# First projections of a decoder-layer kernel: three units side by side, loads in small pieces, and the norm's factor used later

## The chip, the core and the metric

The kernel runs on one core of a Trainium2 chip. The metric is the device time of one execution in microseconds (us). The profile names the engines of a core PE (TensorE, matrix products; PEld are its weight loads), DVE (VectorE), ACT (ScalarE), POOL (GpSimd) and SP (SyncE, which issues the DMA transfers here). Each engine works through its own queue of instructions in a fixed order, and waits where an instruction needs something that another engine or a transfer has not finished.

## What is computed

One inference step of a decoder layer over 336 tokens (16 meta tokens, a prompt of 256, and 8 sequences of 8 tokens), in float32, with a model width of 2048. Cut to what the change touches:

```python
h = rms_norm(x, norm_w)                  # x * rsqrt(mean(x * x) + eps) * norm_w
proj = h @ w_in
z, xbc, dt_raw, sc_b, sc_c, sc_h, sc_z, g_a, g_b = split_proj(proj)
# branch A: causal conv on xbc, chunked state-space scan, gated norm, projection
...
# branch B: short gated convolution
u = sc_c * sc_h
u_c, sconv_new = causal_dwconv(u, sconv_prev, sconv_w)
y_b = (sc_b * u_c * jax.nn.silu(sc_z)) @ w_sconv_out
merged = jax.nn.sigmoid(g_a) * y_a + jax.nn.sigmoid(g_b) * y_b
return x + merged @ w_o, conv_new, state, sconv_new      # then a final rms_norm
```

The change lies in the norm and in the first projections of branch B: sc_b, sc_c, sc_h and sc_z.

## The kernel before

Tokens lie along the columns, features along the 128 partitions. `ya` holds x as 16 tiles (index k) of 128 features by 336 tokens. A *unit* is a projection onto 128 output features: 16 tiles of k, and for each k three products of 128 by 128 weights with up to 336 columns, since float32 factors are split into a high part that PE multiplies in one pass (fp32r) and the low rest: high times high, high times low, low times high. The weights of a unit are two blocks of 128 by 1024; `wblk` loads a block (SP, `wraw`), makes its high part (ACT, `whi`, L83) and its low part (DVE, `wlo`, L85), with three buffers for each. `unit` and `mm` (L88 to L102) issue for each block eight pairs of products with `whi` (L91, L92), and behind them the eight with `wlo` (L95). `w2[j]`, `w2[16+j]`, `w2[32+j]` and `w2[48+j]` are the weights of the units of sc_b, sc_c, sc_h and sc_z.

Of PSUM there are two buffers named `pj`, for units, and two named `ms`, for small sums. The instructions' order on each engine is set by a scheduler when the program is built, from the order in which the code is written and from its own estimates; buffers of pools are reused in turn, and a tile waits until its buffer is free.

The stage that the change touches, in the order of the code (L147 to L258):

- The vectors `V` (192 KB: conv weights, biases, norm weights) are loaded, the pieces of x, and the blocks of the units w2[16] and w2[32]. POOL halves two parts of `V` (L158, L159).
- x times the norm weight, without the norm's factor, is split into `uhi` (ACT, L163) and `ulo` (DVE, L164). Units on `uhi` and `ulo` need no norm factor ahead of them; their results are multiplied by it afterwards.
- Units w2[16] and w2[32] run side by side over k (L166 to L174). `conv_in` copies the first (`c_s`) and multiplies it with the second into `up`.
- The squares of `ya` (ACT, L214) are summed in `sacc` over k by DVE (L216). `rstd` (L107 to L126) adds up over the partitions with three products on `sacc` (L113); DVE and POOL form the inverse root; DVE lays it on diagonals `rs_d` (L123) and three products (L124) spread it to all partitions. From this come `rsb` (ACT, L226) and its square `rs2` (L228).
- Six more units follow on `uhi` and `ulo`, in this order: w2[48], w2[0], w2[17], w2[33], w2[49], w2[1]. `scaled` multiplies the results of w2[48] and w2[49] (`zf`) and of w2[0] and w2[1] (`bf`) by `rsb` (L231); w2[17] is multiplied by `rs2` where it is copied (L184).
- `ya` becomes h itself (L242) and is split into `hhi` (ACT, L243) and `hlo` (DVE, L244). Everything behind works on these.
- The loop over j (L250 to L258) runs the convolution of branch B (`conv_out`) and splits its result. For j = 0 and 1 the units are done already; from j = 2 on they are computed on `hhi` and `hlo`, the first being w2[18].

## Time and profile before

| | |
|---|---|
| median of 3 runs | 1886.39 us (1881.93 to 1890.16) |
| profiled execution | 1888.47 us, span on the core 1886.5 us |
| mean granted clock of PE | 0.994 of full speed |
| busy share of the span | PE 98%, PEld 96%, DVE 61%, ACT 40%, POOL 17% |
| first 9.2 us of the span | PE busy 0.06 us, DMA share 0.77, 255 GB/s |
| 9.2 to 15.4 us | PE busy 5.85 of 6.20 us, DMA share 1.00, 413 GB/s |

Busy time counts instructions at work; an engine that waits for another is idle. In the lists that follow a row has its start in us, its length, the engine, the line, the operation, the tile written and the tiles read, and in brackets how long the engine had been idle and who ended that. "x8" is a run of eight instructions that follow each other.

### The profile page before, as it was taken

How to read it: one execution, taken by the hardware profiler on the slowest of the kernel's cores; microseconds unless marked ns; L12 is line 12 of the kernel's file. 1: busy time of each engine (PE TensorE's matmuls, PEld its weight loads, DVE VectorE, ACT ScalarE, POOL GpSimd, SP SyncE). 2: the span in 40 equal slices, each digit the busy share in tenths (PEclk: the TensorE clock that was granted, in tenths of full speed). 3: DMA queues.
4: the chain of work that ended last, by engine and by line, in shares of the span. 5: the costliest groups of instructions: out<-in, count | busy, mean ns of one | idle time of the engine just before them, and what ended most of it. 6: DMA issues, size and time to landing. Idle time of an engine off the chain costs nothing.

```text
span 1886.5 us, 31941 instructions
## 1 busy us (share of the span) xinstructions
PE 1848.2 (98%) x12830; PEld 1808.8 (96%) x12830; DVE 1150.8 (61%) x1798; ACT 749.9 (40%) x1050; POOL 313.8 (17%) x397
## 2 busy tenths in 40 slices
PE   7999999999999999999999999999999999999996
PEld 7999999999999999999999999999999999999996
DVE  6844444444534336568586876868778687674543
ACT  5433333333333335444453443534435344233432
POOL 0100000000000002131332323222133221300011
PEclk9999999999999999999999999999999999999998
DMA  6444444444444446456464665646656466575553
GB/s 218 139 155 146 148 153 146 147 156 149 145 158 155 157 163 223 155 174 238 151 236 164 204 207 161 234 152 214 205 169 227 138 212 203 169 258 164 176 170 108
DMA packets 108948, 332.26 MB, mean 176 GB/s; under 512 B 12288, under 2 KB 30336, under 8 KB 108800
## 3 DMA queue, kind: packets, MB, share of 16 engines
q1 hardware_dynamic: 108800, 330.22, 53.5%
q8 instruction: 101, 1.65, 0.4%
q14 instruction: 47, 0.39, 0.1%
HBM read 297.29 MB, written 32.88 MB: 175 GB/s over the span
## 4 chain that ended last, share of the span: by engine, by line
PE 62%; DVE 2%; issue 1%; DMA 1%; ACT 0%; POOL 0%; DVEq 0%; ACTq 0%; SPq 0%
PE pj L91 19%; PE pj L92 19%; PE pj L95 19%; PE yb L541 1%; DMA W<-ac_d 1%; PE ms L520 1%; PE sg L482 1%; DVE wlo L85 1%; DVE W L457 1%; PE ms L439 1%; PE sg L545 0%; PE sg L541 0%; PE ms L124 0%; PE ms L594 0%; DVE cacc L378 0%
## 5 line engine op out<-in xcount | busy, mean ns | idle before, releaser
L91 PE MATMUL pj<-hhi,whi 128*128 128x320 f32 (+3 forms) x2960 | 892.8, 313 | 0.3 <-DVE ya L626 0.3
L92 PE MATMUL pj<-hlo,whi 128*128 128x320 f32 (+3 forms) x2960 | 888.3, 312 | 0.0
L85 DVE TENSOR_TENSOR wlo<-wraw,whi 128x1024 fp32r<-128x1024 f32 x481 | 598.6, 1245 | 458.9 <-PE pj L95 263.2
L83 ACT ACTIVATE whi<-wraw 128x1024 fp32r<-128x1024 f32 x481 | 508.9, 1058 | 846.1 <-PE pj L92 764.9
L91 PEld LDWEIGHTS pj<-hhi,whi 128*128 128x128 f32 x2960 | 557.6, 188 | 5.7 <-issue 3.3
L92 PEld LDWEIGHTS pj<-hlo,whi 128*128 128x128 f32 x2960 | 556.9, 188 | 0.3
L95 PE MATMUL pj<-hhi,wlo 128*128 128x320 f32 (+3 forms) x2960 | 501.4, 312 | 0.0
L95 PEld LDWEIGHTS pj<-hhi,wlo 128*128 128x128 f32 x2960 | 455.8, 188 | 0.3
L91 PE MATMUL pj<-yh,whi 128*128 128x320 f32 x512 | 156.9, 319 | 0.0
L92 PE MATMUL pj<-yl,whi 128*128 128x320 f32 x512 | 152.2, 309 | 0.0
L91 PEld LDWEIGHTS pj<-yh,whi 128*128 128x128 f32 x512 | 96.5, 188 | 7.8 <-issue 5.9
L92 PEld LDWEIGHTS pj<-yl,whi 128*128 128x128 f32 x512 | 96.4, 188 | 1.4 <-issue 1.4
L95 PE MATMUL pj<-yh,wlo 128*128 128x320 f32 x512 | 95.9, 310 | 0.0
L378 DVE SCALAR_TENSOR_TENSOR cacc<-pad,V,cacc 128x360 f32<-128x360 f32 (+1 forms) x144 | 85.0, 590 | 7.4 <-ACT cacc L376 5.6
L626 DVE TENSOR_TENSOR ya<-ya,pj 128x320 f32<-128x320 f32 x112 | 54.2, 484 | 52.7 <-PE pj L95 51.6
L490 POOL TENSOR_TENSOR h<-h,decS 128x512 f32<-128x512 f32 x64 | 72.3, 1166 | 57.3 <-PE ms L520 57.3
L194 POOL COPY SCS<-up 128x2 f32<-128x2 f32 x16 | 19.4, 1215 | 370.9 <-DVE up L188 367.9
L95 PEld LDWEIGHTS pj<-yh,wlo 128*128 128x128 f32 x512 | 80.4, 188 | 0.0
L92 PE MATMUL pj<-vlo,whi 128*128 128x320 f32 x256 | 75.5, 309 | 0.0
L91 PE MATMUL pj<-vhi,whi 128*128 128x320 f32 x256 | 75.5, 309 | 0.0
L371 POOL COPY pad<-cs 128x24 f32<-128x24 f32 x48 | 40.5, 844 | 132.6 <-DVE cacc L378 104.9
L457 DVE TENSOR_SCALAR W<-W,act 128x128 f32<-128x128 f32 (+1 forms) x192 | 54.2, 336 | 6.8 <-DMA W<-ac_d 6.7
(206 smaller groups left out, 1517.9 us busy)
## 6 DMA issues: line engine op xcount, KB each, us to landing
wraw<-w SPq DMA_DIRECT2D x352, 512.0 KB, 3.9
wraw<-wso SPq DMA_DIRECT2D x64, 512.0 KB, 3.5
wraw<-wsc SPq DMA_DIRECT2D x32, 512.0 KB, 3.7
h<-h0T SPq DMA_DIRECT2D x32, 512.0 KB, 5.0
ssms<-h SPq DMA_DIRECT2D x32, 512.0 KB, 4.8
wraw<-wo SPq DMA_DIRECT2D x32, 512.0 KB, 3.8
W<-ac_d SPq DMA_DIRECT2D x16, 512.0 KB, 5.4
xq_d<-xe SPq DMA_DIRECT2D x16, 320.0 KB, 3.5
```

The lines of the kernel that those rows point to most:

```text
L83: nc.scalar.activation(hi[:, :n], raw[:, :n], AF.Copy)
L85: nc.vector.tensor_tensor(lo[:, :n], raw[:, :n], fb(hi[:, :n]), sub)
L91: nc.tensor.matmul(out, w, xh(k0 + k), start=first and k == 0, stop=False)
L92: nc.tensor.matmul(out, w, xl(k0 + k), start=False, stop=False)
L95: nc.tensor.matmul(out, w, xh(k0 + k), start=False, stop=last and k == nk - 1)
L194: nc.gpsimd.tensor_copy(SCS[:, j, 0, :], up[:, 256:258])
L371: nc.gpsimd.tensor_copy(smp[:, :, 0:3], cs[:, 1:9, :])
L378: nc.vector.scalar_tensor_tensor(acc[:, i0:], pad[:, i0 + k:360 + k], col(V_CW, 4 * j + k), acc[:, i0:], mult, add)
L439: nc.tensor.transpose(pp[:n, t * P:t * P + P], xs[:, t, t0:t0 + n], ident)
L457: nc.vector.tensor_scalar(w[:n, h, :n], w[:n, h, :n], act[:n, c, 8 * g + h:8 * g + h + 1], 0.0, sub, ALU.min)
L490: nc.gpsimd.tensor_tensor(split(h0[b]), split(h0[b]), bc(hv(decS[:, b, :], g), [P, 8, HP]), mult)
L626: nc.vector.tensor_tensor(ya[:, m, :TV], ya[:, m, :TV], pp[:, :TV], add)
```

## The change

- *Dummy products.* A tile `warm` is cleared by DVE; ACT reads it once, which loads ACT's function table; PE runs eight products of 128 columns on it into a bank of `ms`.
- *Loads.* Of `V` only the 16 columns of the norm weights come first (8 KB); then a tile of x (168 KB) and 256 columns (128 KB) of each of three blocks, and so on in pieces that grow to two tiles of x and 512 columns. The other parts of `V` come behind all of these. The blocks are split in the same pieces (`wsplit`).
- *Three units side by side.* w2[16], w2[32] and w2[48] run side by side over k; for each k stand the three products of each unit. The third unit's sum lies in a bank of `ms`.
- *Squares.* POOL instead of DVE adds the squares into `sacc`.
- *The factor later.* `rstd` is stopped behind its column sums and the inverse root, the units w2[17] and w2[33] are written ahead of its second half, and w2[0] ahead of its first. w2[48] and w2[0] are copied from PSUM without the factor (ACT) and multiplied in place afterwards (DVE). `up` of the second pair is formed without the factor and multiplied by `rs2` afterwards, as that of the first was.
- *`hlo`.* Every third one is made by POOL instead of DVE (five of 16).

```diff
@@ -22,6 +22,7 @@
 NH = 64
 HP = 64
 EPS = 1e-6
+WARM = 8
 NSTEP = 22
 
 C_ID, C_U, C_M1, C_UQ, C_M1Q, C_ONE = 0, 128, 256, 384, 464, 544
@@ -145,43 +146,68 @@
     CH = ((0, P), (P, P), (2 * P, 80))
 
     with tc.tile_pool(name="pa", bufs=2) as pa:
-        nc.sync.dma_start(V, vec)
-        nc.sync.dma_start(ya[:, 0:2, :], xT[:, 0:2, :])
-        wb = [[wblk(w2[16][:, 0:1024])], []]
-        nc.sync.dma_start(ya[:, 2:4, :], xT[:, 2:4, :])
-        nc.sync.dma_start(ya[:, 4:8, :], xT[:, 4:8, :])
-        wb[1].append(wblk(w2[32][:, 0:1024]))
-        nc.sync.dma_start(ya[:, 8:12, :], xT[:, 8:12, :])
-        wb[0].append(wblk(w2[16][:, 1024:2048]))
-        nc.sync.dma_start(ya[:, 12:16, :], xT[:, 12:16, :])
-        wb[1].append(wblk(w2[32][:, 1024:2048]))
-        nc.gpsimd.tensor_scalar(V[:, V_CW:V_CW + 240], V[:, V_CW:V_CW + 240], 0.5, None, mult)
-        nc.gpsimd.tensor_scalar(V[:, V_SCW:V_SCW + 48], V[:, V_SCW:V_SCW + 48], 0.5, None, mult)
+        warm = pa.tile([P, 256], F32, name="warm", bufs=1)
+        nc.vector.memset(warm, 0.0)
+        nc.scalar.activation(warm[:, 0:1], warm[:, 1:2], AF.Copy)
+        pw = ps.tile([P, 512], F32, name="ms")
+        for _ in range(WARM):
+            nc.tensor.matmul(pw[:, :P], warm[:, P:], warm[:, :P], start=True, stop=True)
         uhi = pa.tile([P, KT, T], F32R, name="uhi", tag="vhi", bufs=1)
         ulo = pa.tile([P, KT, T], F32R, name="ulo", tag="vlo", bufs=1)
+        first = [(w2[16], 14), (w2[32], 14), (w2[48], META)]
+        wb = [tuple(wp.tile([P, 1024], d, name=n) for n, d in (("wraw", F32), ("whi", F32R), ("wlo", F32R)))
+              for _ in first]
+        pu = [ps.tile([P, 512], F32, name=n) for n in ("pj", "pj", "ms")]
+
+        def lw(a, b):
+            for (src, _), (raw, hi, lo) in zip(first, wb):
+                o = slice(a % 1024, a % 1024 + b - a)
+                nc.sync.dma_start(raw[:, o], src[:, a:b])
+
+        def lx(a, b):
+            nc.sync.dma_start(ya[:, a:b, :], xT[:, a:b, :])
+
+        def wsplit(a, b):
+            for raw, hi, lo in wb:
+                o = slice(a % 1024, a % 1024 + b - a)
+                nc.scalar.activation(hi[:, o], raw[:, o], AF.Copy)
+                nc.vector.tensor_tensor(lo[:, o], raw[:, o], fb(hi[:, o]), sub)
+
+        nc.sync.dma_start(V[:, V_NW:V_NW + KT], vec[:, V_NW:V_NW + KT])
+        lx(0, 1)
+        lw(0, 256)
+        lx(1, 2)
+        lw(256, 512)
+        lx(2, 4)
+        lw(512, 1024)
+        lx(4, 6)
+        lx(6, 8)
+        edge = {0: (0, 256), 2: (256, 512), 4: (512, 1024), 8: (1024, 1536), 12: (1536, 2048)}
         for k in range(KT):
             nc.scalar.activation(uhi[:, k, :], ya[:, k, :], AF.Copy, scale=col(V_NW, k))
             nc.vector.scalar_tensor_tensor(ulo[:, k, :], ya[:, k, :], col(V_NW, k), fb(uhi[:, k, :]), mult, sub)
-
-        pu = [ps.tile([P, 512], F32, name="pj") for _ in range(2)]
-        for half in range(2):
-            for k in range(8):
-                for i in range(2):
-                    hi, lo = wb[i][half]
-                    kk = 8 * half + k
-                    for j, (w, x) in enumerate(((hi, uhi), (hi, ulo), (lo, uhi))):
-                        nc.tensor.matmul(pu[i][:, :T - 14], w[:, k * P:k * P + P], x[:, kk, 14:],
-                                         start=kk == 0 and j == 0, stop=kk == 15 and j == 2)
+            if k in edge:
+                wsplit(*edge[k])
+            if k in (4, 8):
+                lx(k + 4, k + 6)
+                lw(*edge[k + 4])
+                lx(k + 6, k + 8)
+            for (_, t0), p, (raw, hi, lo) in zip(first, pu, wb):
+                for j, (w, x) in enumerate(((hi, uhi), (hi, ulo), (lo, uhi))):
+                    o = k % 8 * P
+                    nc.tensor.matmul(p[:, :T - t0], w[:, o:o + P], x[:, k, t0:],
+                                     start=k == 0 and j == 0, stop=k == 15 and j == 2)
+        nc.sync.dma_start(V[:, 0:V_NW], vec[:, 0:V_NW])
+        nc.sync.dma_start(V[:, V_NW + KT:], vec[:, V_NW + KT:])
+        nc.gpsimd.tensor_scalar(V[:, V_CW:V_NW], V[:, V_CW:V_NW], 0.5, None, mult)
+        nc.gpsimd.tensor_scalar(V[:, V_SCW:V_SCW + 48], V[:, V_SCW:V_SCW + 48], 0.5, None, mult)
 
         def uproj(src, t0):
             return unit(src, lambda k: uhi[:, k, t0:T], lambda k: ulo[:, k, t0:T], T - t0)
 
-        def conv_in(j, pr, pre=None, fac=None):
+        def conv_in(j, pr, pre=None):
             c_s = pa.tile([P, T - 14], F32, name="c_s")
-            if fac is None:
-                nc.scalar.activation(c_s, pre[0] if pre else pr(w2[16 + j], 14), AF.Copy)
-            else:
-                nc.vector.tensor_tensor(c_s, pr(w2[16 + j], 14), fac, mult)
+            nc.scalar.activation(c_s, pre[0] if pre else pr(w2[16 + j], 14), AF.Copy)
             ph = pre[1] if pre else pr(w2[32 + j], 14)
             up = pa.tile([P, 338], F32, name="up")
             ups = eights(up[:, 258:338], 10)
@@ -207,13 +233,13 @@
                                     mult)
             return th
 
-        up0, ups0 = conv_in(0, None, [p[:, :T - 14] for p in pu])
+        up0, ups0 = conv_in(0, None, [p[:, :T - 14] for p in pu[:2]])
         sacc = pa.tile([P, T], F32, name="sacc", bufs=1)
         for k in range(KT):
             sq = pa.tile([P, T], F32, name="sq") if k else sacc
             nc.scalar.activation(sq, ya[:, k, :], AF.Square)
             if k:
-                nc.vector.tensor_tensor(sacc, sacc, sq, add)
+                nc.gpsimd.tensor_tensor(sacc, sacc, sq, add)
 
         def consts(a, b):
             craw = wp.tile([P, 1024], F32, name="craw", tag="wraw")
@@ -221,19 +247,26 @@
             nc.vector.tensor_copy(CR[:, a:b], craw[:, :b - a])
 
         consts(0, C_SE)
-        rs = run(rstd(pa, [sacc], 0, 1.0 / DM, EPS))
+        zf = [pa.tile([P, TV], F32, name="zf", bufs=1)]
+        nc.scalar.activation(zf[0], pu[2][:, :TV], AF.Copy)
+        bf = [pa.tile([P, TV], F32, name="bf", bufs=1)]
+        nc.scalar.activation(bf[0], uproj(w2[0], META), AF.Copy)
+        norm = rstd(pa, [sacc], 0, 1.0 / DM, EPS)
+        next(norm)
+        up1, ups1 = conv_in(1, uproj)
+        rs = run(norm)
         rsb = pa.tile([P, T], F32, name="rsb", bufs=1)
         nc.scalar.activation(rsb, rs, AF.Copy)
         rs2 = pa.tile([P, T], F32, name="rs2", bufs=1)
         nc.vector.tensor_tensor(rs2, rsb, rs, mult)
+        for f in (zf[0], bf[0]):
+            nc.vector.tensor_tensor(f, f, rsb[:, META:], mult)
+
         def scaled(w, name, **kw):
             f = pa.tile([P, TV], F32, name=name, **kw)
             nc.vector.tensor_tensor(f, uproj(w, META), rsb[:, META:], mult)
             return f
 
-        zf = [scaled(w2[48], "zf", bufs=1)]
-        bf = [scaled(w2[0], "bf", bufs=1)]
-        u1 = conv_in(1, uproj, fac=rs2[:, 14:])
         zf.append(scaled(w2[49], "zf1", tag="sq"))
         bf.append(scaled(w2[1], "bf1", tag="sq"))
         nc.sync.dma_start(SCS, sconvst)
@@ -241,14 +274,15 @@
             hf = ya[:, k, :]
             nc.vector.scalar_tensor_tensor(hf, hf, col(V_NW, k), rsb, mult, mult)
             nc.scalar.activation(hhi[:, k, :], hf, AF.Copy)
-            nc.vector.tensor_tensor(hlo[:, k, :], hf, fb(hhi[:, k, :]), sub)
-        nc.vector.tensor_tensor(up0[:, :258], up0[:, :258], rs2[:, 14:272], mult)
-        nc.vector.tensor_tensor(ups0[:, :, 2:10], ups0[:, :, 2:10], eights(rs2[:, 272:]), mult)
+            (nc.gpsimd if k % 3 == 2 else nc.vector).tensor_tensor(hlo[:, k, :], hf, fb(hhi[:, k, :]), sub)
+        for u_, us in ((up0, ups0), (up1, ups1)):
+            nc.vector.tensor_tensor(u_[:, :258], u_[:, :258], rs2[:, 14:272], mult)
+            nc.vector.tensor_tensor(us[:, :, 2:10], us[:, :, 2:10], eights(rs2[:, 272:]), mult)
 
         vhi = pa.tile([P, KT, TV], F32R, name="vhi", bufs=1)
         vlo = pa.tile([P, KT, TV], F32R, name="vlo", bufs=1)
         for j in range(KT):
-            u = (up0, ups0) if j == 0 else u1 if j == 1 else conv_in(j, proj)
+            u = (up0, ups0) if j == 0 else (up1, ups1) if j == 1 else conv_in(j, proj)
             if j == 3:
                 nc.sync.dma_start(HV, hvec)
                 consts(C_SE, C_ALL)
```

How the order on the engines changes. PE before, from the end of the first pairs of products of w2[0] on (`sacc` holds the summed squares, `rs_d` the factor's diagonals):

```order
L91 MATMUL pj<-uhi,whi 128x320
L92 MATMUL pj<-ulo,whi 128x320
L113 MATMUL ms<-CR,sacc 112x1 x3
L95 MATMUL pj<-uhi,wlo 128x320 x5
L124 MATMUL ms<-rs_d,CR 128x112 x2
L95 MATMUL pj<-uhi,wlo 128x320 x2
L124 MATMUL ms<-rs_d,CR 128x112
L95 MATMUL pj<-uhi,wlo 128x320
L91 MATMUL pj<-uhi,whi 128x320
```

PE now, from the end of the three units on, and, in the second list, around the use of the factor:

```order
L198 MATMUL pj<-uhi,wlo 128x322
L198 MATMUL ms<-uhi,whi 128x320
L198 MATMUL ms<-ulo,whi 128x320
L198 MATMUL ms<-uhi,wlo 128x320
L114 MATMUL ms<-CR,sacc 112x1 x3
L92 MATMUL pj<-uhi,whi 128x320
L93 MATMUL pj<-ulo,whi 128x320
```

```order
L92 MATMUL pj<-uhi,whi 128x322
L93 MATMUL pj<-ulo,whi 128x322
L96 MATMUL pj<-uhi,wlo 128x322 x8
L125 MATMUL ms<-rs_d,CR 128x112 x2
L92 MATMUL pj<-uhi,whi 128x320
L93 MATMUL pj<-ulo,whi 128x320
```

The column sums stand right behind the three units now, ahead of all of w2[0]; before they stood behind its first 16 products. Between them and the first use of `rs_d` lie now the units w2[0], w2[17] and w2[33] instead of five products. The third product on `rs_d` stands two pairs further on.

POOL before, behind its start, and now:

```order
L158 ISA
L158 TENSOR_SCALAR V<-V 128x240
L159 TENSOR_SCALAR V<-V 128x48
L193 COPY up<-SCS 128x8x2 x2
L118 TENSOR_TENSOR rs_r<-rs_m,mhalf 112x3
```

```order
L242 ISA
L242 TENSOR_TENSOR sacc<-sacc,sq 128x336 x9
L202 TENSOR_SCALAR V<-V 128x240
L203 TENSOR_SCALAR V<-V 128x48
L242 TENSOR_TENSOR sacc<-sacc,sq 128x336 x6
L219 COPY up<-SCS 128x8x2 x2
L119 TENSOR_TENSOR rs_r<-rs_m,mhalf 112x3
L277 TENSOR_TENSOR hlo<-ya,hhi 128x336 x5
```

The 15 additions are new on POOL; the two scalings of `V` stand behind nine of them, the inverse root `rs_r` behind all, and five `hlo` behind that.

ACT now, from the end of the splits of x on (L173 is a piece of the three blocks, L84 a block behind them; `c_s` copies the unit w2[16], `zf` the unit w2[48]):

```order
L173 ACTIVATE whi<-wraw 128x512
L240 ACTIVATE sq<-ya 128x336
L187 ACTIVATE uhi<-ya,V 128x336 x2
L240 ACTIVATE sq<-ya 128x336 x6
L84 ACTIVATE whi<-wraw 128x1024
L210 ACTIVATE c_s<-pj 128x322
L251 ACTIVATE zf<-ms 128x320
L84 ACTIVATE whi<-wraw 128x1024 x2
L303 ACTIVATE na<-HV 64x1
L84 ACTIVATE whi<-wraw 128x1024 x2
L253 ACTIVATE bf<-pj 128x320
```

and ACT before, at the same place:

```order
L83 ACTIVATE whi<-wraw 128x1024
L214 ACTIVATE sq<-ya 128x336
L182 ACTIVATE c_s<-pj 128x322
L214 ACTIVATE sq<-ya 128x336
L83 ACTIVATE whi<-wraw 128x1024
L214 ACTIVATE sq<-ya 128x336 x2
L269 ACTIVATE na<-HV 64x1
L83 ACTIVATE whi<-wraw 128x1024
L214 ACTIVATE sq<-ya 128x336 x2
L83 ACTIVATE whi<-wraw 128x1024
```

The last six squares stood between whole blocks' splits before; now they stand in a row ahead of the first of these, and of the copy that frees a bank of `pj`.

DVE before, at the first `wlo` for a unit on `hhi` (the first of the row of two; `uc` and `thz` are the convolution of branch B for j = 0 and 1, `up` what it starts from):

```order
L197 TENSOR_SCALAR uc<-up,V 128x336
L205 TENSOR_TENSOR thz<-thz,uc 128x256
L206 TENSOR_TENSOR thz<-thz,uc 128x64
L198 SCALAR_TENSOR_TENSOR uc<-up,V,uc 128x336
L203 SCALAR_TENSOR_TENSOR thz<-thz,zf_588 128x320
L199 SCALAR_TENSOR_TENSOR uc<-up,V,uc 128x336
L85 TENSOR_TENSOR wlo<-wraw,whi 128x1024 x2
L231 TENSOR_TENSOR bf_651<-pj,rsb 128x320
L258 TENSOR_TENSOR vlo<-thz,vhi 128x320
L204 TENSOR_TENSOR thz<-thz,bf_651 128x320
L85 TENSOR_TENSOR wlo<-wraw,whi 128x1024
```

and now, up to the first `wlo` for a unit on `hhi`:

```order
L225 SCALAR_TENSOR_TENSOR uc<-up,V,uc 128x336
L223 TENSOR_SCALAR uc<-up,V 128x336
L231 TENSOR_TENSOR thz<-thz,uc 128x256
L232 TENSOR_TENSOR thz<-thz,uc 128x64
L224 SCALAR_TENSOR_TENSOR uc<-up,V,uc 128x336
L229 SCALAR_TENSOR_TENSOR thz<-thz,zf_626 128x320
L292 TENSOR_TENSOR vlo<-thz,vhi 128x320
L225 SCALAR_TENSOR_TENSOR uc<-up,V,uc 128x336
L230 TENSOR_TENSOR thz<-thz,bf_689 128x320
L86 TENSOR_TENSOR wlo<-wraw,whi 128x1024
```

What stood behind that `wlo`, the second gate `bf_689`, its products and the first `vlo`, stands ahead of it now.

## The prediction, made before the changed kernel ran

> **What bounds the kernel now.** I read the page's engine line first, then the list of what PE waited for, then PE's rows in order of time.
>
> ```profile
> span 1886.5 us, 31941 instructions
> ...
> PE 1848.2 (98%) x12830; PEld 1808.8 (96%) x12830; DVE 1150.8 (61%) x1798; ACT 749.9 (40%) x1050; POOL 313.8 (17%) x397
> ```
>
> The waits of PE (us in total, times, longest):
>
> ```profile
> PE pj L173 <- ACT whi L83: 9.1, 1, 9.1
> ...
> PE ms L113 <- DVE sacc L216: 1.6, 1, 1.6
> ```
>
> PE is busy for 98% of the span. A change at the front can win only PE's idle or slow time there: 9.1 us before the first product, 1.6 us before the norm's column sums, and what the rows in order of time show beside them (start, length, what it waited for):
>
> ```profile
> 9.14 0.64 PE L173 MATMUL pj<-uhi,whi 128*128 128x322 f32 x1 [9.14 <-ACT whi L83]
> ...
> 15.12 0.47 PE L173 MATMUL pj<-ulo,whi 128*128 128x322 f32 x1
> 15.39 0.39 PE L173 MATMUL pj<-uhi,whi 128*128 128x322 f32 x1
> ...
> 17.54 0.31 PE L173 MATMUL pj<-uhi,whi 128*128 128x322 f32 x1
> 17.69 0.31 PE L173 MATMUL pj<-ulo,whi 128*128 128x322 f32 x1
> ...
> 32.59 1.33 PE L95 MATMUL pj<-uhi,wlo 128*128 128x320 f32 x8
> ...
> 37.90 0.75 PE L113 MATMUL ms<-CR,sacc 128*112 128x1 f32 x6 [1.63 <-DVE sacc L216]
> 40.18 1.20 PE L124 MATMUL ms<-rs_d,CR 112*128 112x112 f32 x4 [0.69 <-DVE rs_d L123]
> 41.06 0.88 PE L95 MATMUL pj<-uhi,wlo 128*128 128x320 f32 x2
> 41.73 0.60 PE L124 MATMUL ms<-rs_d,CR 112*128 112x112 f32 x2
> ...
> 46.16 0.36 PE L91 MATMUL pj<-uhi,whi 128*128 128x320 f32 x1
> ...
> 75.93 0.31 PE L91 MATMUL pj<-hhi,whi 128*128 128x322 f32 x1
> ```
>
> Products start 0.27 us apart until 15.39 and 0.15 apart after it: the first 6.25 us run at half rate. The third unit ends at 33.9 (32.59 and 1.33). 75.93 is the first product on hhi; I measure everything at that point, because behind the work it starts the order of all engines is the same again. From 9.14 to 75.93 PE took 66.8 us for 384 products (56.8 at 0.148) and the norm's six small ones (1.3). So 8.7 us are lost to waits and slow clock, beside the 9.1 ahead of them. That is all there is to win. The clock, in windows of 2 us (PE, PEld, DVE, ACT and POOL busy, granted clock, DMA share, GB/s):
>
> ```profile
> 36.00:38.00 2.00, 0.37 (x3) 0.11 (x3) 1.74 (x3) 1.36 (x2) 0.00 (x0) 1.00 0.60 223
> ...
> 42.00:44.00 2.00, 2.00 (x9) 2.00 (x9) 1.28 (x2) 0.45 (x1) 0.00 (x0) 0.50 0.00 0
> 1110.00:1112.00 2.00, 0.36 (x4) 0.12 (x2) 1.97 (x4) 1.16 (x2) 1.06 (x1) 1.00 0.61 223
> 1112.00:1114.00 2.00, 1.65 (x12) 1.65 (x13) 2.00 (x5) 0.89 (x3) 0.01 (x1) 1.00 0.40 125
> 1460.00:1462.00 2.00, 0.47 (x5) 0.47 (x5) 2.00 (x4) 1.77 (x3) 1.07 (x1) 1.00 0.49 193
> 1462.00:1464.00 2.00, 2.00 (x12) 2.00 (x11) 1.97 (x5) 0.28 (x1) 0.17 (x1) 0.70 0.72 229
> ```
>
> A stall of about 1.6 us is followed by half clock twice (after 36 and after 1460) and once not (after 1110). Once slow, PE worked from 40.18 to 46.16 before it was fast again: 6.0 us at half rate, a loss of 3.0.
>
> **The start.** How loads, ACT and the table load stood before, with the time of V's load from issue to landing:
>
> ```profile
> 1.65 0.43 SPq L81 DMA_DIRECT2D wraw<-w  x1
> 2.12 0.43 SPq L151 DMA_DIRECT2D ya<-xT  x1
> ...
> 4.26 1.28 ACT L163 ACT_TABLE_LOAD   x1 [4.26 <-DMA ya<-xT]
> 5.56 0.57 ACT L163 ACTIVATE uhi<-ya,V 128x336 fp32r<-128x336 f32 x1
> ...
> 8.03 1.06 ACT L83 ACTIVATE whi<-wraw 128x1024 fp32r<-128x1024 f32 x1 [1.89 <-DMA wraw<-w]
> 14.70 1.97 ACT L163 ACTIVATE uhi<-ya,V 128x336 fp32r<-128x336 f32 x4
> ```
>
> ```profile
> V<-vec SPq DMA_DIRECT2D x1, 192.0 KB, 2.4
> ```
>
> SP issues a DMA every 0.47 us. The three pieces of 128 KB are issued third to fifth, from 1.65 to 2.6; with V's 2.4 they land at 4.1 to 5.0. The table load now waits for nothing and ends near 2.1 instead of 5.54, so uhi, a square and the first split of 256 columns are done near 4.8. The eight dummy products start when the table is there, near 2.3. Two of L124's (112 columns) took 0.88 at half clock, 40.18 to 41.06, so eight of 128 columns take 4.0. Real work starts at 6.3: the dummies hold it for 1.5, and it is 2.8 earlier than 9.14. If it takes 6.25 us to the full rate again, PE is slow until 8.6, and real work loses 1.1.
>
> The loads, in a slice where several overlapped (columns as above):
>
> ```profile
> 7.00:8.00 1.00, 0.00 (x0) 0.00 (x0) 0.00 (x0) 0.00 (x0) 0.00 (x0) 1.00 1.03 416
> ```
>
> Three units are 144 products, 21.3 us. Their loads are 5.9 MB; at the rate of this slice that is 14.2 us, less than PE's work, and I allow 0.8 for the early k that wait for theirs:
>
> The units end at 6.3 + 1.1 + 21.3 + 0.8 = 29.5, which is 4.4 before 33.9. SP issues 27 loads for this instead of 10; the 17 more cost 8 us on a queue that waits for tiles to come free anyway.
>
> **The squares.** 15 additions go from DVE to POOL. The nearest rows of POOL (min/median/max in ns for L699, the same addition at the end of the program, and for L582; else a mean), and ACT's square:
>
> ```profile
> L699 POOL TENSOR_TENSOR sacc<-sacc,sqf x14: 878/1153/1437, 1771.2 to 1863.1; 128x320 f32<-128x320 f32 x14
> L582 POOL TENSOR_TENSOR zs<-zs x24: 879/890/1492, 827.3 to 1636.5; 128x320 f32<-128x320 f32 x24
> ...
> L158 POOL TENSOR_SCALAR V<-V 128x240 f32<-128x240 f32 x1 | 0.8, 815 | 2.8 <-DMA V<-vec 2.8
> L159 POOL TENSOR_SCALAR V<-V 128x48 f32<-128x48 f32 x1 | 0.3, 327 | 0.0
> ```
>
> ```profile
> L214 ACT ACTIVATE sq<-ya 128x336 f32<-128x336 f32 x15 | 6.7, 474 | 0.4 <-DVE sacc L216 0.4
> ```
>
> For 336 columns and a handoff I take 1.05, between the medians 0.89 and 1.15, with 0.9 and 1.5 as bounds. Nine additions stand ahead of the two scalings of V and six behind them. ACT's instructions follow each other 0.09 faster than they last (four uhi in 1.97 instead of 2.26). Ahead of the end of the tenth square ACT has 14 uhi at 0.47, ten squares at 0.38, and six splits of 256 and nine of 512 columns (0.32 and 0.53 each, between 0.474 for 336 and 1.06 for 1024): 17.1 us from 3.4, with 2.3 of waits for first loads, so 22.8. POOL ends its ninth addition at 24.2, the scalings at 25.3, the other six at 31.6. PE's column sums stand right behind the three units, so PE idles from 29.5 to 31.6: 2.1 us, between 1.2 at 0.9 and 4.8 at 1.5. Behind PE's wait stands all of w2[0]. The last squares wait for POOL to free one of two buffers, and behind them on ACT stand the next split and the copy c_s that frees a PSUM buffer; these end near 31.4, inside the same wait.
>
> **The factor wanted later.** Between the column sums and the use of their result lie three units now, 21 us, against a chain of under 4 (37.90 to 41.73); the wait of 0.69 and the slow stretch to 46.16 go. From 31.6 PE has 240 products (35.4) and the six small ones (1.2): hhi at 68.2. Whether the 2.1 of idle brings half clock is open, by the windows above; half of 3.0 gives 69.7, which is 6.2 ahead of 75.93.
>
> **What is late next.** DVE makes ya, hlo and the splits' low parts:
>
> ```profile
> 43.87 0.50 DVE L228 TENSOR_TENSOR rs<-rsb,ms 128x336 f32<-128x336 f32 x1
> ...
> 47.89 0.49 DVE L231 TENSOR_TENSOR bf<-pj,rsb 128x320 f32<-128x320 f32 x1 [1.21 <-PE pj L95]
> ...
> 49.43 1.76 DVE L244 TENSOR_TENSOR hlo<-ya,hhi 128x336 fp32r<-128x336 f32 x4
> ...
> 74.13 2.36 DVE L85 TENSOR_TENSOR wlo<-wraw,whi 128x1024 fp32r<-128x1024 f32 x2
> ```
>
> From rs2 (43.87) to the first wlo for hhi (74.13) DVE took 30.3 us, 28.7 of them work. In the new order that stretch loses five wlo of the other units (1.13 each, 5.7), five hlo that go to POOL (0.42 each, 2.1) and c_s and up of the second pair (0.9); it gains up1's scaling, bf1, one vlo and one thz, which stood behind that wlo (1.7): 21.7. rs2 starts 1.0 behind the last L125 (rsb and a handoff), and the wlo itself takes 1.2: 23.9 behind it. PE has by then 92 products and the 32 on hhi that need no wlo: 18.3. So PE idles 5.6 us at its first wlo product on hhi (4 to 7). Before, 34.2 us lay between (41.73 to 75.93). The stall is three times the one that brought half clock, so I add 3.0 less what of it passes in the wait: 2.5.
>
> At nothing: c_s goes from DVE to ACT (0.44 us, ACT is 40% busy); V's other pieces land by 20, ahead of POOL's scaling at 24.2, and without that cover POOL and with it PE would wait; POOL's five hlo fit between ACT's hhi.
>
> **Sum.** Work on hhi begins 6.2 earlier, its wlo costs 5.6, the clock 2.5: 1.9 later. The profiled execution of 1888.47 (span 1886.5) would be 1890.4. It lies 2.1 above the median shown, 1886.39, so I predict 1888.
>
> The Trainium skill, TensorE: Matmul & The Clock Gate, section HAM oscillation, has PE slow down only after idle gaps over about 3.4 us. The trace does not agree: 1.63 us was enough at 37.90. By that rule the 2.1 us idle would cost no clock, and the sum would be 0.4 later instead of 1.9.
>
> **Rivals.** The slice in which the first loads of before landed:
>
> ```profile
> 4.00:5.00 1.00, 0.00 (x0) 0.00 (x0) 0.00 (x0) 0.73 (x1) 0.37 (x2) 1.00 0.84 205
> ```
>
> (a) DVE is in time and PE flows into hhi: 5.6 and 2.5 go, 6.2 earlier, 1880. For it: DVE was in time before. Against it: the lead is 18.3 where 23.9 are due. (b) POOL's additions stretch beside DVE, and PE waits longer for the column sums. For it: L582 once took 1.49. At 1.5, six additions add 2.7 and make half clock sure (1.5): 1892. From 2.1 an addition (six times 1.05 more, 1.5 and 1.9) it alone makes the kernel slower by over 0.5%. (c) Small loads move less. At the 205 GB/s of this slice 5.9 MB take 29 us from 2.3; the units end at 32.5, POOL's chain too is 3 later: 1891.
>
> The Trainium skill, DMA: Bandwidth & Descriptors, section Bandwidth, speaks for (c): it asks for 1 MiB in one DMA and gives 64 KB a third of the peak. The trace speaks against it: loads of 336 to 672 KB that overlapped reached 416.
>
> **Chances.** Forecast 0.74, by itself 1884 to 1892 (1.2 to 4.8 of POOL, the clock's luck); (a) 0.10, (b) 0.09, (c) 0.07. The range, 1880 to 1894, takes in the centres of all and leaves out the far half of (a) and the tail of (b). Under 0.5%, 9.4 us, a measurement of this kernel tells no change from none. Even with both of PE's waits away some 9 is the most to win: faster 0.06, same 0.89, slower 0.05.
>
> **What would show it.** Real products from about 6; three units done near 29.5; a wait of PE for POOL's sacc of about 2; none for rs_d; a wait of some 5 for DVE's wlo on hhi near 75, then a clock of 0.5. The prediction is wrong if PE flows into hhi, or if loads starve the first k.

## The result, and the profile after

The changed kernel took 1896.26 us (median of 6 runs, 1891.58 to 1897.99) against 1886.5 before (6 runs): a ratio of 1.0051, 95% interval 1.0034 to 1.0068, so slower by about 9.6 us. The forecast was 1888 within 1880 to 1894 and no change; slower by over 0.5% had a chance of 0.05. One execution of run e11 below, 2754.89 us at a granted clock of 0.608, is in none of the ratios.

The span of the profiled execution and what PE waited for (us in total, times, longest):

```profile
span 1895.6 us, 32037 instructions
...
PE 1852.5 (98%) x12846; PEld 1812.4 (96%) x12846; DVE 1154.0 (61%) x1789; ACT 753.5 (40%) x1063; POOL 337.6 (18%) x417
```

```profile
PE pj L96 <- DVE wlo L86: 7.5, 1, 7.5
...
PE pj L198 <- ACT uhi L187: 3.7, 2, 2.7
...
PE ms L154 <- ACT warm L151: 2.3, 1, 2.3
...
PE ms L114 <- POOL sacc L242: 1.5, 1, 1.5
```

The wait at the start fell from 9.1 to 2.3, and the one for the sum of the squares (1.6 before) is still there with 1.5. The waits for uhi and for a wlo are new, the latter a single one of 7.5. PE's rows in order of time show where (start, length, what it waited for):

```profile
2.28 3.78 PE L154 MATMUL ms<-warm 128*128 128x128 f32 x16 [2.28 <-ACT warm L151]
5.71 0.61 PE L198 MATMUL pj<-uhi,whi 128*128 128x322 f32 x1
...
10.50 0.56 PE L198 MATMUL pj<-uhi,whi 128*128 128x322 f32 x2 [0.95 <-ACT uhi L187]
...
16.32 0.56 PE L198 MATMUL pj<-uhi,whi 128*128 128x322 f32 x2 [2.71 <-ACT uhi L187]
...
19.41 0.47 PE L198 MATMUL pj<-uhi,wlo 128*128 128x322 f32 x1
19.68 0.47 PE L198 MATMUL pj<-uhi,whi 128*128 128x322 f32 x1
...
34.02 0.31 PE L198 MATMUL ms<-uhi,wlo 128*128 128x320 f32 x1
35.81 0.75 PE L114 MATMUL ms<-CR,sacc 128*112 128x1 f32 x6 [1.48 <-POOL sacc L242]
...
74.06 0.31 PE L92 MATMUL pj<-hhi,whi 128*128 128x322 f32 x1
...
86.87 2.51 PE L96 MATMUL pj<-hhi,wlo 128*128 128x322 f32 x8 [7.50 <-DVE wlo L86]
```

The real work began 3.4 us earlier than before (5.71 against 9.14), but the three units ended at 34.33 (34.02 and 0.31) instead of 33.9: PE was dry twice, and ran at half clock (0.27 between starts at 19.41) behind the second time. ACT's rows show that the uhi it waited for were waiting for loads:

```profile
9.88 1.05 ACT L187 ACTIVATE uhi<-ya,V 128x336 fp32r<-128x336 f32 x2 [0.39 <-DMA ya<-xT]
...
13.91 0.63 ACT L173 ACTIVATE whi<-wraw 128x512 fp32r<-128x512 f32 x1 [1.86 <-DMA wraw<-w]
...
15.69 1.04 ACT L187 ACTIVATE uhi<-ya,V 128x336 fp32r<-128x336 f32 x2 [0.22 <-DMA ya<-xT]
```

Work on hhi began only 1.9 earlier (74.06 against 75.93); then came the wait of 7.5 with half clock behind it. From windows of 5.2 and 3.2 us (PE, PEld, DVE, ACT, POOL busy, granted clock, DMA share, GB/s):

```profile
86.80:92.00 5.20, 5.13 (x19) 5.13 (x20) 3.16 (x6) 1.53 (x2) 3.22 (x1) 0.50 0.59 184
92.00:95.20 3.20, 3.20 (x23) 3.20 (x22) 1.26 (x2) 1.13 (x2) 0.00 (x0) 1.00 0.81 256
```

About 5 us at half rate lose 2.5. So 7.5 + 0.2 (a short wait for hhi) + 2.5 - 1.9 = 8.3 of the 9.1 between the two profiled spans stand in this stage.

### The profile page after: what moved, and what is told of

It reads as the page before. It is cut to its first block, busy times and chain, and to the rows that moved or that the text cites. A ratio compares the mean times of both kernels' runs of the same rounds, so it can differ in the third digit from the quotient of the medians.

```text
span 1895.6 us, 32037 instructions
## 1 busy us (share of the span) xinstructions
PE 1852.5 (98%) x12846; PEld 1812.4 (96%) x12846; DVE 1154.0 (61%) x1789; ACT 753.5 (40%) x1063; POOL 337.6 (18%) x417
## 4 chain that ended last, share of the span: by engine, by line
PE 62%; DVE 3%; issue 1%; ACT 0%; DMA 0%; POOL 0%; DVEq 0%; ACTq 0%
PE pj L92 19%; PE pj L93 19%; PE pj L96 19%; PE yb L575 1%; DVE wlo L86 1%; PE ms L554 1%; PE sg L516 1%; DVE W L491 1%; PE ms L473 1%; PE sg L579 0%; PE sg L575 0%; PE ms L125 0%; DVE cacc L412 0%; PE ms L628 0%; DMA W<-ac_d 0%
## 5 line engine op out<-in xcount | busy, mean ns | idle before, releaser
L86 DVE TENSOR_TENSOR wlo<-wraw,whi 128x1024 fp32r<-128x1024 f32 x475 | 592.1, 1247 | 463.7 <-PE pj L96 269.3
L84 ACT ACTIVATE whi<-wraw 128x1024 fp32r<-128x1024 f32 x475 | 502.6, 1058 | 840.3 <-PE pj L93 763.7
```

What stands on the lines that cost most here:

```text
L84: nc.scalar.activation(hi[:, :n], raw[:, :n], AF.Copy)
L86: nc.vector.tensor_tensor(lo[:, :n], raw[:, :n], fb(hi[:, :n]), sub)
```

## The experiments

Ratios are to the kernel before, run beside each experiment; its median was 1880 beside e1 to e4, 1885 beside e5 to e8 and 1883 beside e9 to e12, so only ratios are set against each other. They are not quotients of the medians, from which they differ by up to 0.0008 (that of e5 is 1.0049), so smaller differences between them say nothing.

| run | units end | sums at | first on hhi | wait at first wlo on hhi | ratio, 95% interval |
|---|---|---|---|---|---|
| before | 33.9 | 37.90 | 75.93 | 0 | 1 |
| changed kernel | 34.33 | 35.81 | 74.06 | 7.50 | 1.0051 (1.0034 to 1.0068) |
| e5, the same again | 33.75 | 35.17 | 71.86 | 7.52 | 1.0054 (1.0039 to 1.0068) |
| e1 hlo on DVE | 34.26 | 35.82 | 74.06 | 7.10 | 1.0062 (1.0039 to 1.0084) |
| e2 conv work later | 33.55 | 34.94 | 73.16 | 2.52 | 1.0034 (1.0022 to 1.0045) |
| e3 squares on DVE | 33.70 | 33.54 | 70.25 | 7.54 | 1.0019 (1.0002 to 1.0036) |
| e4 larger first loads | 32.28 | 37.19 | 76.09 | 7.54 | 1.0070 (1.0044 to 1.0097) |
| e6 factor before w2[17] | 34.22 | 35.61 | 73.33 | 0.95 | 1.0020 (1.0007 to 1.0032) |
| e7 start only | 32.15 | 32.11 | 69.27 | 0 | 0.9975 (0.9957 to 0.9992) |
| e8 no dummies | 33.90 | 35.34 | 72.03 | 7.53 | 1.0042 (1.0024 to 1.0059) |
| e9 later factor only | 33.06 | 39.91 | 69.48 | 7.04 | 1.0009 (0.9990 to 1.0027) |
| e10 start, squares on POOL | 33.72 | 35.07 | 73.24 | 0 | 0.9987 (0.9971 to 1.0004) |
| e11 start, larger loads | 32.02 | 32.36 | 69.50 | 0 | 0.9979 (0.9960 to 0.9998) |
| e12 factor one unit later | 33.96 | 33.80 | 72.42 | 0 | 0.9994 (0.9976 to 1.0011) |

(Times in us in one profiled execution of each.)

**e1: hlo on DVE again.**

```diff
-            (nc.gpsimd if k % 3 == 2 else nc.vector).tensor_tensor(hlo[:, k, :], hf, fb(hhi[:, k, :]), sub)
+            nc.vector.tensor_tensor(hlo[:, k, :], hf, fb(hhi[:, k, :]), sub)
```

> All 16 hlo on DVE again, the rest as in the changed kernel. There DVE needed 24.3 us from rs2 (61.26) to the first wlo for hhi (85.60), and PE waited 7.5 for it. Theory (DVE and POOL hold each other up): while POOL worked on its five hlo, DVE's ya and hlo took 3.1 us longer in sum than at 0.51 and 0.45 each; they fall back to that, DVE gets five hlo of 0.45 = 2.3 more: the wait is 6.7, and the time the same within 1. Rival (POOL's help is free): the wait grows by 2.3 to 9.8, and the time by 2.3.

The wait was 7.10: nearer to the theory (6.7) than to the rival (9.8). The rows of ya in the changed kernel and in e1 (min/median/max in ns, first and last start), a hlo on POOL with the ya beside it, and DVE's first wlo for hhi in both:

```profile
L275 DVE SCALAR_TENSOR_TENSOR ya<-ya,V,rsb x16: 553/560/1219, 62.5 to 78.1; 128x336 f32<-128x336 f32 x16
...
L277 POOL TENSOR_TENSOR hlo<-ya,hhi x5: 993/1127/2072, 64.9 to 77.9; 128x336 fp32r<-128x336 f32 x5
...
72.82 2.07 POOL L277 TENSOR_TENSOR hlo<-ya,hhi 128x336 fp32r<-128x336 f32 x1 [3.14 <-ACT hhi L276]
74.03 2.18 DVE L275 SCALAR_TENSOR_TENSOR ya<-ya,V,rsb 128x336 f32<-128x336 f32 x3
...
85.60 1.22 DVE L86 TENSOR_TENSOR wlo<-wraw,whi 128x1024 fp32r<-128x1024 f32 x1
```

```profile
L275 DVE SCALAR_TENSOR_TENSOR ya<-ya,V,rsb x16: 549/556/561, 62.5 to 77.1; 128x336 f32<-128x336 f32 x16
...
73.02 1.51 DVE L275 SCALAR_TENSOR_TENSOR ya<-ya,V,rsb 128x336 f32<-128x336 f32 x3
...
84.76 1.21 DVE L86 TENSOR_TENSOR wlo<-wraw,whi 128x1024 fp32r<-128x1024 f32 x1
```

With POOL at work single ya took up to 1219 ns, without it none over 561. DVE with five hlo more came to the wlo 0.84 sooner: POOL's five hlo spared DVE 2.1 and made its other rows some 2.9 longer. The help of POOL was worth less than nothing to DVE; the time itself (1.0062) can't be told from the changed kernel's.

**e2: the third pair's units ahead of the first convolutions.**

```diff
-            up = pa.tile([P, 338], F32, name="up")
+            up = pa.tile([P, 338], F32, name="up", bufs=3)
...
-            u = (up0, ups0) if j == 0 else (up1, ups1) if j == 1 else conv_in(j, proj)
+            if j == 0:
+                u2 = conv_in(2, proj)
+            u = ((up0, ups0), (up1, ups1), u2)[j] if j < 3 else conv_in(j, proj)
```

> The two units of the third pair are written ahead of the convolutions of j = 0 and 1 (up gets a third buffer); the first three wlo for hhi then stand on DVE ahead of uc and thz. Theory (DVE's order makes the wlo late): the wlo starts behind up's scaling, at 80.5 instead of 85.6; PE's wait falls from 7.5 to 2.4, and the half clock behind it (about 2.5 us lost) may go too: 1889 to 1891. Rival (the wlo waits for its whi or for a buffer, not for DVE's turn): the wait stays near 7, 1896.

```profile
80.98 2.44 PE L96 MATMUL pj<-hhi,wlo 128*128 128x322 f32 x8 [2.52 <-DVE wlo L86]
```

The wait fell to 2.52, as the theory had it (2.4), and the rival's 7 did not come: the wlo was late because of what stood ahead of it on DVE. In time it was 1.0034, some 3 to 4 us less than the changed kernel, where 5 to 7 were expected; the clock behind the wait still went to half for a short while (starts 0.27 apart from 83.2 to 84.3).

**e3: the squares on DVE again.**

```diff
-                nc.gpsimd.tensor_tensor(sacc, sacc, sq, add)
+                nc.vector.tensor_tensor(sacc, sacc, sq, add)
```

> The 15 additions of squares on DVE again, the rest as in the changed kernel. There ulo took 1.0 and a wlo of 512 columns 1.2 while POOL added, against 0.55 and 0.69 before it began. Theory (they hold each other up, and POOL's additions are the slower way): both fall back, ACT's last squares wait for nothing, PE's wait of 1.5 for sacc goes, work on hhi starts about 2 earlier, a little more if the half clock at 37.4 goes too: 1892 to 1894. Rival (DVE is too full in this stage): wlo and ulo come later than PE wants them, the three units end later than 34.3: 1898.

```profile
33.54 0.66 PE L114 MATMUL ms<-CR,sacc 128*112 128x1 f32 x6
```

The sums stand right behind the units now, without a wait, and work on hhi begins 3.8 earlier than in the changed kernel's profile (1.6 earlier than in e5's). The wait of 7.54 at the wlo stayed. The units ended at 33.70, as in e5 (33.75), and not later, as the rival had it. The time was 1.0019 against 1.0051 and 1.0054: 4 to 6 us less, where 2 to 4 were expected. The stage shows 1.6 to 3.8 of them; where the rest was won isn't shown. The rows of ulo, in the changed kernel and in e3, and of POOL's additions in the changed kernel:

```profile
L188 DVE SCALAR_TENSOR_TENSOR ulo<-ya,V,uhi x16: 555/566/1225, 4.5 to 29.7; 128x336 fp32r<-128x336 f32 x16
...
L242 POOL TENSOR_TENSOR sacc<-sacc,sq x15: 895/1043/2147, 7.9 to 34.9; 128x336 f32<-128x336 f32 x15
```

```profile
L188 DVE SCALAR_TENSOR_TENSOR ulo<-ya,V,uhi x16: 555/561/687, 4.6 to 26.6; 128x336 fp32r<-128x336 f32 x16
```

**e4: larger first loads.**

```diff
-        lx(0, 1)
-        lw(0, 256)
-        lx(1, 2)
-        lw(256, 512)
+        lx(0, 2)
+        lw(0, 512)
         lx(2, 4)
         lw(512, 1024)
-        lx(4, 6)
-        lx(6, 8)
-        edge = {0: (0, 256), 2: (256, 512), 4: (512, 1024), 8: (1024, 1536), 12: (1536, 2048)}
+        lx(4, 8)
+        edge = {0: (0, 512), 4: (512, 1024), 8: (1024, 1536), 12: (1536, 2048)}
```

> The first loads in larger pieces: two tiles of x, 512 columns of each block, again two tiles and 512, then four tiles of x; behind k = 8 as in the changed kernel. Theory (small pieces move slowly: 157 to 251 GB/s between 3 and 8 us with the DMA engines 80 to 100% busy, against 350 to 407 later): the first real product comes at 6 to 7 instead of 5.7, the idle times of 0.95 and 2.71 shrink to under 1 in sum, the clock stays full, and the three units end near 31.5 instead of 34.3; the time falls by 2 to 3. Rival (three blocks for each k are simply more bytes than arrive, whatever the pieces): the idle times stay, the units end at 34.3 or later, and the time is the same or 1 longer.

The units ended 1.5 to 2 sooner (32.28), but the order of ACT and POOL moved with the splits: nine of the 15 additions came last.

```profile
37.19 1.28 PE L114 MATMUL ms<-CR,sacc 128*112 128x1 f32 x6 [4.91 <-POOL sacc L239]
```

What the loads won was lost to POOL's additions, and more: 1.0070. On the units the theory was nearer (31.5 against the rival's 34.3 or later), though PE still idled 1.98 for loads and ran at half rate from 7.1 to 11.1; it missed the next wait.

**e5: the changed kernel again.**

> The changed kernel once more, beside the others of this set on the same chip, so that they can be set against it: 9 to 10 slower than before on this chip too, a ratio of 1.0045 to 1.0055.

A median of 1893.88 beside 1884.59, with a ratio of 1.0054, as expected. Its wait of 1.42 for the sums was not followed by half clock, that of 1.48 in the first profile was (starts 0.27 apart from 37.4 to 39.8). Its hhi began 2.2 earlier, at 71.86: 0.6 of that stands already at the sums (35.17 against 35.81), the other 1.6 is the clock.

**e6: the factor ahead of w2[17] and w2[33].**

```diff
-        up1, ups1 = conv_in(1, uproj)
         rs = run(norm)
...
+        up1, ups1 = conv_in(1, uproj)
+
         def scaled(w, name, **kw):
```

> The second half of the norm is written ahead of w2[17] and w2[33] instead of behind them, so that PE's products on rs_d stand behind w2[0] alone; all else as in the changed kernel. There DVE was idle for 2.3 us of each 3.5 while PE worked at w2[17] and w2[33], since the factor wasn't there yet, and was late by 7.5 afterwards. Theory (the factor comes too late for DVE, which has 24 us of work to do behind it): PE needs rs_d near 45, when it is ready (40.4); rs2 comes near 47 instead of 61.3, PE has 30 us of products until it wants the first wlo for hhi instead of 18, and the wait of 7.5 goes to under 1, with the half clock behind it (2.5): 9 to 10 less than the changed kernel, about the time of before. Rival (DVE is late because its work beside POOL is too much for this stage, whenever it starts): the wait moves to another wlo or hlo, and less than half is won.

PE's wait at the wlo fell from 7.5 to 0.95, without half clock behind it: the theory's mechanism. In the set of e5 the median fell by 5.6 us only (1893.88 to 1888.31), not 9 to 10; the profiled execution of 1883.01 was among the fastest of the 12 (1882.04 to 1892.64). What the slower ones lost isn't shown.

**e7: the new start with the old rest.** Dummies, loads and three units as in the changed kernel; from the squares on the kernel before, with w2[48] scaled from its bank of ms:

```diff
-        zf = [scaled(w2[48], "zf", bufs=1)]
+        zf = [pa.tile([P, TV], F32, name="zf", bufs=1)]
+        nc.vector.tensor_tensor(zf[0], pu[2][:, :TV], rsb[:, META:], mult)
```

> The new start (dummies, small loads, three units side by side) with the kernel before behind it: squares added by DVE, factor used at once, hlo on DVE. Theory: the start itself wins 0 to 2 us, since PE idles for loads and runs at half clock for it: units done at 33.5 to 34.3 against 33.9 before; behind it the wait for rs_d and a slow stretch as before, no wait at the first wlo for hhi: ratio 0.999 to 1.001. Rival (the start's loads and splits also disturb what follows, or it is the start that lost the 9 us): 1.003 or more.

```profile
15.75 0.56 PE L198 MATMUL pj<-uhi,whi 128*128 128x322 f32 x2 [1.73 <-ACT uhi L187]
...
32.11 0.72 PE L114 MATMUL ms<-CR,sacc 128*112 128x1 f32 x6
...
36.33 0.67 PE L125 MATMUL ms<-rs_d,CR 112*128 112x112 f32 x4 [0.33 <-DVE rs_d L124]
```

Faster than before: 0.9975, interval 0.9957 to 0.9992, better than the theory (0.999 to 1.001). Two things that the theory counted on did not come in this profile: half clock behind the idle time of 1.73, and the slow stretch behind the sums, where PE waited only 0.33 for rs_d. In the other kernels with the same loads the idle time at this place (1.66 to 2.71) was followed by half clock, and their units ended at 33.5 to 34.3.

**e8: no dummies.**

```diff
-WARM = 8
+WARM = 0
```

> No dummy products; the early table load stays; all else as in the changed kernel. Theory (loads bound PE up to 16 us, so a clock that is slow until then is hidden): the first real product comes near 5.2 at half clock, the idle times of 0.95 and 2.71 shrink, the three units end within 0.7 of 34.3, and the time is the same as that of the changed kernel. Rival (the dummies' clock is worth its price): the units end 2 to 3 later, and the time is as much longer.

1892.22, 1.0042, not to be told from e5. Real products began at 5.39 at half clock, the wait at 10.5 was gone, and the units ended at 33.90 against 33.75 in e5. What the dummies win in clock is lost again in waits for loads.

**e9: the later factor alone**, on the kernel before (diff shortened; `zf`, `bf` and both `up` are scaled afterwards as in the change):

```diff
-        rs = run(rstd(pa, [sacc], 0, 1.0 / DM, EPS))
+        zf = [pa.tile([P, TV], F32, name="zf", bufs=1)]
+        nc.scalar.activation(zf[0], uproj(w2[48], META), AF.Copy)
+        bf = [pa.tile([P, TV], F32, name="bf", bufs=1)]
+        nc.scalar.activation(bf[0], uproj(w2[0], META), AF.Copy)
+        norm = rstd(pa, [sacc], 0, 1.0 / DM, EPS)
+        next(norm)
+        up1, ups1 = conv_in(1, uproj)
+        rs = run(norm)
```

> The kernel before with the later factor alone: its start, its loads, squares and hlo on DVE; w2[48] and w2[0] copied without the factor, w2[17] and w2[33] ahead of the products on rs_d. Theory (it is the later factor that makes DVE late): no wait for sacc or rs_d and no slow stretch at 40 to 46, so work on hhi starts at 70 to 71 instead of 75.93; but PE then waits 6.5 to 7.5 for the first wlo, with 1.5 to 2.5 of half clock behind it: 2 to 5 slower than before, a ratio of 1.001 to 1.003. Rival (the later factor is good by itself and the rest spoils it): no wait above 2, a ratio of 0.997 to 0.998.

```profile
69.48 0.31 PE L92 MATMUL pj<-hhi,whi 128*128 128x322 f32 x1
...
81.44 2.51 PE L96 MATMUL pj<-hhi,wlo 128*128 128x322 f32 x8 [7.04 <-DVE wlo L86]
```

Without the new start and without POOL's help the wait of 7 is there: it belongs to the later factor. Work on hhi began 6.45 earlier (69.48 against 75.93), 0.9 of which stands already at the end of the units (33.06 against 33.9), and the wait gave back 7.0 and some clock. The time, 1.0009 with an interval of 0.9990 to 1.0027, is not to be told from before, nor from the theory's 1.001 to 1.003; the rival's 0.997 to 0.998 is excluded.

**e10: e7 with the squares on POOL.**

```diff
-                nc.vector.tensor_tensor(sacc, sacc, sq, add)
+                nc.gpsimd.tensor_tensor(sacc, sacc, sq, add)
```

> As the run with the new start alone (e7: units done at 32.15, sums at 32.11, work on hhi from 69.27), but the squares are added by POOL. Theory (POOL's additions and DVE's work of two inputs hold each other up): ulo and wlo take about twice as long from 20 to 30, the additions end 1.3 to 1.6 behind the units, the sums stand at 34.5 to 35.8 and work on hhi starts 2 to 4 later than in e7: ratio 0.999 to 1.001. Rival (the squares' place matters little, as DVE has time): within 1 of e7.

Sums at 35.07 behind a wait of 1.35, hhi at 73.24, 4.0 later than in e7, as the theory had it (2 to 4). The time, 0.9987, lies between theory (0.999 to 1.001) and rival, and can't be told from e7's. Of the 4.0, 1.6 stand already at the end of the units (half clock from 16.8 to 19.5), a delay that e3 and e12 (units at 33.70 and 33.96) show with squares on DVE too. POOL's part is the wait and the clock behind it.

**e11: e7 with the larger loads of e4** (the same edit).

> The new start alone (e7) with the larger first pieces of the run e4. Theory (larger pieces bring the bytes sooner): first real product at 6.7, one idle time of under 1.4 near 15 instead of 0.63 and 1.73, units done at 30.5 to 31.5 instead of 32.15, and the time 1 less than e7 where the sums don't wait: ratio 0.9965 to 0.9975. Rival (DVE now has eight additions in a row at the end): PE waits 1 or more for sacc and what is won is lost again, ratio 0.9975 to 0.999.

Units at 32.02, sums behind a wait of 0.34, 0.9979: the same as e7. PE's idle times only moved. How much the loads brought (same columns; before, the changed kernel, e11):

```profile
6.00:10.00 4.00, 0.86 (x2) 0.50 (x2) 1.45 (x2) 2.11 (x5) 0.00 (x0) 1.00 1.02 408
10.00:14.00 4.00, 3.65 (x14) 3.61 (x14) 4.00 (x9) 4.00 (x10) 0.00 (x0) 1.00 1.03 423
```

```profile
6.00:10.00 4.00, 3.39 (x19) 2.79 (x17) 3.13 (x6) 2.85 (x8) 0.93 (x1) 1.00 0.97 280
10.00:14.00 4.00, 3.11 (x18) 2.68 (x18) 1.74 (x3) 2.02 (x5) 0.98 (x1) 1.00 0.99 307
```

```profile
6.00:10.00 4.00, 2.47 (x11) 1.49 (x10) 1.80 (x3) 2.16 (x5) 0.00 (x0) 1.00 0.98 290
10.00:14.00 4.00, 3.62 (x23) 3.44 (x24) 3.55 (x7) 3.78 (x8) 0.00 (x0) 1.00 1.02 390
```

The DMA engines were equally busy in all three (0.97 to 1.03), but the changed kernel's pieces of 128 to 336 KB moved 280 to 307 GB/s where before's of 336 to 672 KB moved 408 to 423. In e11, where no piece of x or of the blocks is under 256 KB, the loads moved 290 from 6 to 10 us and 390 from 10 to 14.

**e12: the factor one unit later**, behind w2[0], with squares and hlo on DVE (the edits of e1, e3 and e6 together).

> The changed kernel with squares and hlo on DVE and with the norm's second half behind w2[0] instead of behind w2[33]; the new start stays. Against e7 only the factor is wanted one unit later. Theory (DVE has time enough if it gets the factor near 45): no wait for sacc and none over 0.5 for rs_d or for the first wlo, ratio 0.996 to 0.998, as e7. Rival (any delay of the factor makes DVE late for hhi): a wait of 1 to 3 at the first wlo on hhi, ratio 0.998 to 1.0.

```profile
45.02 0.47 PE L125 MATMUL ms<-rs_d,CR 112*128 112x112 f32 x2 [1.70 <-DVE rs_d L124]
```

There was no wait at the wlo; instead the third rs_d stood on DVE behind a wlo that waited for its whi, and PE waited 1.70 for it. 0.9994: in the rival's range, but without the rival's wait. The lowest ratio is that of e7, which uses the factor at once; those of e11 and e10 can't be told from it.

## Why the prediction was wrong

**Where the time lay: right.** 8.3 of the 9.1 us stand in the stage that the prediction worked through, and each of the waits that it named was there.

**The start: wrong, and the largest miss.** "The units end at 6.3 + 1.1 + 21.3 + 0.8 = 29.5" failed in its last term, and through it in its second. It took the rate of 416 from large loads as that of the small ones, and set the sum of the loads against the sum of the products. By each k there was no slack: a k needs 0.37 MB (5.9 by 16), an estimated 1.3 us at 280 GB/s, and its nine products take 1.33. PE idled 3.8 (0.16, 0.95, 2.71) instead of 0.8. Of 34.33, 5.71 is the start (the dummies held it 0.3 longer than in e8, not 1.5), 21.3 the products at full rate and 3.8 idle. Of the 3.5 that are left, 1.9 are half clock behind the second idle time (15 products from 16.32 to 20.41) and 0.5 the slow clock behind the dummies, where 1.1 was forecast for all; about 1.1 is spread over the restarts of PE behind its waits. Rival (c) named the mechanism, but priced only its own 3 us and kept the rest of the sum, giving 1891 and a chance of 0.07. DMA: Bandwidth & Descriptors, in the Trainium skill, section Bandwidth, was set aside on the strength of 336 to 672 KB loads; its rule that small DMAs move less agrees with 280 to 307 against 408 to 423 here. That the size of the pieces alone made the loads late isn't shown: with larger ones (e11) the units ended no sooner than in e7.

**POOL's additions: right in size, partly by luck, and late in place.** A wait of 2.1 was forecast and 1.48 found, 1.35 to 1.56 in all but e4 of the kernels with squares on POOL. It starts at 34.3 and not at 29.5, so hhi began at 74.06, not 69.7. The size fits because both ends of the wait moved. POOL's ninth addition ended at 27.9 where 24.2 was forecast (its own terms, 22.8 and 1.05, give 23.9); only the last six took the 6.3 of the forecast:

```profile
25.69 2.25 POOL L242 TENSOR_TENSOR sacc<-sacc,sq 128x336 f32<-128x336 f32 x2 [0.72 <-ACT sq L240]
...
29.43 6.33 POOL L242 TENSOR_TENSOR sacc<-sacc,sq 128x336 f32<-128x336 f32 x6
```

Rival (b), additions stretched beside DVE, came true in part: single ones took up to 2147 ns where 1043 is the median.

**DVE's lateness at the wlo: right in kind, 1.9 too small.** 21.7 was forecast from rs2 to the wlo; 24.3 was measured (61.26 to 85.60). The failed term is "five hlo that go to POOL (0.42 each, 2.1)". e1 shows it: with all hlo on DVE the stretch takes 23.5 (61.27 to 84.76), so POOL's help cost 0.8 where 2.1 was to be won. The row that shows the mechanism is the ya of 1219 ns above. The Trainium skill, SBUF — State Buffer, section Who interferes with whom, says that a DVE instruction with two SBUF inputs contends with a GpSimd instruction that reads SBUF, and that the ports they share are an exclusive lock. The traces fit: a ya took up to 1219 ns where 560 is its median, a hlo on POOL up to 2072 where 993 is its least, about two ya more. The prediction didn't weigh it.

**The clock behind the sums and the wlo: right.** 2.5 was forecast behind the stall, 2.5 measured; half of 3.0 behind the sums, and half clock came there in the first profile and not in e5. The reading beneath it was wrong: of the three stalls "of about 1.6 us" only that before 37.90 is one (1.63). PE's rows give a wait of 2.00 ending at 1112.35, not followed by half clock, and one of 2.52 ending at 1461.53, which was; windows of 2 us show a part of each.

**The sum.** The forecast's 1.9 later becomes 8.4 by the start (4.4 at hhi, 74.06 against 69.7) and the wlo's wait (1.9 more, and 0.2 for a hhi).

**What the parts were worth.** The new start wins (e7), and with the squares on POOL it is not to be told from before (e10, interval up to 1.0004); the later factor loses what it wins (e9); e6 and e2 take most of the wlo's wait away by order alone. Against the changed kernel, the squares on DVE (e3) and the earlier factor (e6) win 4 to 6 us each, and both together with all hlo on DVE (e12) 9 to 11. So more than one part made the kernel slower: by these runs, whose intervals leave some 3 us either way, about half is the factor, put off until DVE, which works behind it, became the bound, and about half the squares on POOL (on the rest of e7 they cost about 2, e10, which isn't clear of the noise).

## What to carry to other kernels

Putting off a value frees the engine that wanted it and delays the one that works behind it: count the second engine's work from the value to its next deadline before moving it. Work given to GpSimd wasn't off VectorE here, where both read two inputs from SBUF (five hlo made VectorE's stretch 0.8 us longer, e1); count it as VectorE's. Price small loads by a row of small loads, and set the loads of each step against the products of that step, not sum against sum.

## What the runs showed of the hardware

Up to 2.7 us the length of a wait of PE did not by itself decide in these runs whether the clock fell to half behind it. It fell after waits of 1.35 (e10), 1.39 (e2) and 1.48 us (the changed kernel's sums), and did not after 1.39 (e6), 1.42 (e5), 1.44 (e8) and 1.73 (e7). Later in the changed kernel it stayed full (granted clock 1.00 from 1356 to 1362) behind a wait of 2.54:

```profile
1356.34 0.33 PE L473 MATMUL ms<-CR,xs 128*128 128x128 f32 x1 [2.54 <-DVE xs L416]
```

Every wait of 4.9 to 7.5 was followed by half clock. Between two profiles of one kernel this moved the start of the work on hhi by 1.6 us. The Trainium skill, TensorE: Matmul & The Clock Gate, section HAM oscillation, puts the gap at over 3.4 us; the waits of 4.9 and more agree, those of 1.35 to 2.7 that were followed by half clock don't.
